# More seven-product pairs in the FFN down projections of a two-layer trunk, with weight parts and residual parked in DRAM

## The chip, the cores and the metric

The kernel runs on one core of one Trainium2 chip. The metric is device time in microseconds of one execution, the median of several runs; lower is better. Engines are named as in the profile: PE (TensorE, matrix products, with PEld its weight loads), DVE (VectorE), ACT (ScalarE), POOL (GpSimd) and SP (SyncE, which here only issues DMAs). Matrix products accumulate in PSUM, eight banks of 128 x 512 float32.

## The reference

Two layers over 256 positions of width 2048. Each layer is a token mixer (a gated MLP with spatial mixing in layer 0, latent attention in layer 1) and a gated FFN with a short causal convolution; each of the four sub-layers ends with a layer norm over the residual sum. What matters here:

```python
def layer_norm(x, g, b):
    mu = jnp.mean(x, axis=-1, keepdims=True)
    var = jnp.mean(jnp.square(x - mu), axis=-1, keepdims=True)
    return (x - mu) * lax.rsqrt(var + LN_EPS) * g + b

def conv_ffn(x, w_up, conv_w, conv_b, w_down):
    h = x @ w_up                                   # 2048 -> 2 * 5504
    h = causal_depthwise_conv(h, conv_w) + conv_b  # width 3
    a, g = jnp.split(h, 2, axis=-1)
    return (jax.nn.silu(g) * a) @ w_down           # 5504 -> 2048

for i in range(2):
    x = layer_norm(ALPHA * x + mixer_i(x), ln_mix_g[i], ln_mix_b[i])
    x = layer_norm(ALPHA * x + conv_ffn(x, ...), ln_ffn_g[i], ln_ffn_b[i])
```

All of it is in float32, and about 470 MB of weights are read once.

## The kernel before

*Products.* A float32 operand is split into a high part (a cast to fp32r, done by ACT) and a low part (operand minus high part, done by DVE). A product is three matmuls: high x high, low x high and high x low.

*Weights.* They come in the order of use as chunks of 1 MiB through SP's queue into a pool `big` of 22 slots of 1 MiB; the activations and the residual live in this pool too. `Feed` keeps the chunk list: `_load` (L76) issues the DMA into a tile `raw`, `_split` (L94) makes the parts `wh` and `wl` (L107, L108), `next` hands out the parts of the chunk now due and lets loads and splits run ahead of it.

*Up projection.* `ffn` runs 21 groups gi. A group takes four chunks (gi 21: two), each for four of the 16 k-tiles, into four banks; the convolution, the gate and the product `act` follow on ACT and DVE (L311, L313, L727 to L745).

*Down projection.* `down` takes its 43 k-tiles as 21 pairs and a single, in two halves of 1024 output columns (`halves`, in an order given by `BACK`). A pair is done for both 128-row blocks b and both 512-column pieces, in one of two ways. `eight` (a wide pair) takes the eight block products, 24 matmuls, into the four banks `DIRECT` = q3, p2, e, q4 (rows b=0 in the first two). `seven` uses the Strassen-Winograd scheme with seven block products, 21 matmuls; it needs sums of blocks of x (`Sums.make`, `combine`) and of the weights (`Feed._seven`: tile `ts`, and the parts wh, wl of 1536 columns and th, tl of 2048, L115 to L122), and four more banks `OWN`. When the last seven pair of a half is through, `rest` combines these banks and `fold` adds them into the residual. In the FFN, pairs 4, 10, 16, 22, 30 and 34 of each half are seven pairs. The last `SKEW` units of the second half are kept for `end(b, f)`, which runs them bank by bank.

*Residual and norm.* `Norm` holds the residual as two tiles of [128, 2048], one for each b, which stay in the pool through the up projection. `piece` adds a bank to the residual and takes its statistics; `start` makes mean and reciprocal deviation; `scale` normalises a piece (L574) and `put` transposes it (bank `lnt`, L587) and splits it into the next stage's operand `xhl` (L591, L594, L595). `boundary` writes out the order of these steps between a stage's end and the first group of the next (`upf` for an up projection, `mq` for the attention's first projection). Since `put` applies gain and bias only to the transposed copy, `restore` applies them to the residual later, in gi 3 to 10 or in the loop after mq, from tiles `lng` and `lnb` of 1 MiB each. In the last norm, `scale` applies gain and bias too (L576, L577) and stores to `out`.

*Order.* The code gives program order; a scheduler then orders the instructions of each engine and each DMA queue by its own estimates when the kernel is built, so the order on an engine can differ from that of the source. Slots of a pool are handed over by waits that it inserts.

Of the kernel before, what the change touches and what calls it, by code (L numbers as in the profile page):

```python
# [15 lines left out]
P = 128  # L16
# [38 lines left out]

BACK = {NF_GM: ((4, 10, 16, 22, 28, 34, 40), (11, 1, 2, 0, 4, 5, 7, 8, 10, 3, 6, 9), (5, 8)),
        NF_FF: ((4, 10, 16, 22, 30, 34), (10, 1, 2, 0, 4, 5, 7, 8, 3, 6, 9), ())}

# [10 lines left out]
class Feed:  # L69

    def __init__(self, nc, pool, chunks):
        self.nc, self.pool, self.chunks = nc, pool, chunks
        self.raw, self.parts = {}, {}
        self.loaded = self.split = self.used = 0  # L76

    def _load(self):
        ap, cols = self.chunks[self.loaded][:2]
        t = self.pool.tile([P, 2048], F32, tag="big", name=f"raw{self.loaded}")  # L80
        step = 512 if self.loaded == 0 else cols
        if len(ap.shape) == 3:
            self.nc.sync.dma_start(t.rearrange("p (k c) -> p k c", k=ap.shape[1]), ap)
        else:
            if self.loaded in (1, 2):
                step = 1024
            for o in range(0, cols, step):
                self.nc.sync.dma_start(t[:, o : o + step], ap[:, o : o + step])
                if self.loaded == 0 and o == step:
                    self.between[0]()  # L90
        self.raw[self.loaded] = t
        self.loaded += 1

    def _split(self):  # L94
        i = self.split
        cols, kind = self.chunks[i][1:]
        raw = self.raw.pop(i)
        if kind == "seven":
            self.parts[i] = self._seven(i, raw)
            self.split += 1  # L100
            return
        hi = self.pool.tile([P, 2048], F32R, tag="big", name=f"wh{i}")
        lo = self.pool.tile([P, 2048], F32R, tag="big", name=f"wl{i}")
        step = 512 if i == 0 else cols if kind == "wide" and i > 2 else 1024 if cols == 2048 else cols // 2
        for o in range(0, cols, step):
            c = slice(o, o + step)
            self.nc.scalar.copy(hi[:, c], raw[:, c])  # L107
            self.nc.vector.tensor_tensor(lo[:, c], raw[:, c], hi[:, c].bitcast(F32), ALU.subtract)  # L108
# [9 lines left out]
    def _seven(self, i, raw):  # L118
# [31 lines left out]
def trunk(ctx: ExitStack, tc: tile.TileContext, x, xT, gm_in, gm_wout, ffn_up, ffn_dn,  # L150
# [6 lines left out]
    st = ctx.enter_context(tc.tile_pool(name="st", bufs=4))  # L157
    ps = ctx.enter_context(tc.tile_pool(name="ps", bufs=8, space=bass.MemoryType.PSUM))

    def slot(shape, name, dt=F32):  # L160
# [8 lines left out]

    chunks = []  # L170
    n_up = ffn_up.shape[1]
# [5 lines left out]
    def back(w, n_k):  # L177

        for hf, units in enumerate(halves(n_k)):
            c = slice(hf * 1024, (hf + 1) * 1024)  # L180
            for u in units:
                if len(u) == 1:
                    chunks.append((w[u[0], :, c], 1024, "wide"))
                else:
                    chunks.append((w[u[0] : u[0] + 2, :, c].rearrange("k p c -> p k c"), 2048,
                                   "seven" if u[0] in BACK[n_k][0] else "wide"))

# [10 lines left out]

    feed = Feed(nc, big, chunks)

# [208 lines left out]
    def down(n_k, src, tag, ln, sums, skew=SKEW):  # L409


        ln.begin()
        quads, sevens = sums.quads, BACK[n_k][0]
        late = []
        for hf, units in enumerate(halves(n_k)):
# [5 lines left out]
            for i, u in enumerate(units):  # L421
# [94 lines left out]
    class Norm:  # L516


        def __init__(self, idx, res, last=False):
            self.idx, self.res, self.last, self.new = idx, res, last, None  # L520
            self.folded = set()

        def begin(self):
            if self.res is None:
                self.res = []
                for b in range(2):
                    t = slot([P, D], f"res{b}")
                    nc.sync.dma_start(t, x[b * P : (b + 1) * P, :])
                    self.res.append(t)
# [12 lines left out]

        def restore(self, b, f):

            c = slice(f * 512, (f + 1) * 512)
            r = self.res[b][:, c]
            nc.vector.tensor_tensor(r, r, self.g[:, c], ALU.mult)
            nc.vector.tensor_tensor(r, r, self.b[:, c], ALU.add)

        def fold(self, b, f, part):  # L550

            r = self.res[b][:, f * 512 : (f + 1) * 512]
            nc.vector.scalar_tensor_tensor(r, r, ALPHA, part, ALU.mult, ALU.add)
            self.folded.add((b, f))

        def piece(self, b, f, acc):
            r = self.res[b][:, f * 512 : (f + 1) * 512]
            if (b, f) in self.folded:
# [11 lines left out]
        def scale(self, b, f):  # L570
            c = slice(f * 512, (f + 1) * 512)
            r = self.res[b][:, c]
            if not self.last:
# [6 lines left out]
        def put(self, b, f):  # L580
# [4 lines left out]
            for j in range(4):  # L585
                o = f * 512 + j * P
                nc.tensor.transpose(t[:, j * P : (j + 1) * P], self.res[b][:, o : o + P], ident)  # L587
            y = tp.tile([P, 4, P], F32, tag="t2", name=f"lny{i}_{b}_{f}", bufs=6)
# [128 lines left out]

    ln = Norm(0, None)
    acc, end = down(NF_GM, pT, "wo", ln, sums)


# [12 lines left out]
    def ffn(layer, ln, acc, end, last):  # L734
# [25 lines left out]
        boundary(ln, acc, end, f"upf{layer}_", after)  # L760
        xhl, res = ln.new, ln.res
# [21 lines left out]
        ln = Norm(2 * layer + 1, res, last)  # L783
        return (ln, *down(NF_FF, act, f"dn{layer}", ln, sums, 4 if last else SKEW))
# [61 lines left out]
    xhl, res = ln.new, ln.res  # L846
    ln.rows()
    kvp = [(0, KVR // 2), (KVR // 2, KVR // 2)]
    acc = [[bank(f"mkv{b}_{f}") for f in range(2)] for b in range(2)]
    for c in range(6):  # L850
# [8 lines left out]
        if 1 <= c < 5:  # L859
            for f in range(2 * ((c - 1) % 2), 2 * ((c - 1) % 2) + 2):  # L860
                ln.restore((c - 1) // 2, f)
    kr2 = []
# [297 lines left out]
```

## Time and profile before

| what | value |
|---|---|
| runs | median 2494.65 us (2493.96 to 2495.05, three runs) |
| profiled execution | span 2492.6 us |
| PE, DVE, ACT, POOL busy | 2478.0, 1886.7, 1381.9, 2.9 us |
| DMA | 480.27 MB, mean 193 GB/s, 54.3% of 16 engines' span in the one queue of loads |
| granted PE clock | full in all 40 slices |
| layer 0's FFN | up projection to 1286.4 us, down projection 1286.4 to 1512.7 us |
| layer 1's FFN | down projection 2256.4 to 2482.2 us, then the last norm and the stores |

The span is the time from the first to the last instruction of the profiled execution; the runs are timed apart from it. An operand written `wl<-raw,wh 128x1024` means that the tile wl is written from raw and wh, in 128 partitions of 1024 elements. In the chain of waits each row is a stretch of the work that ended last, with start and length. In a view of windows each engine has its busy time in the stretch and its instruction count.

### The profile page before, as it was taken

To read this page: it belongs to the slowest core of one execution; us is meant where nothing else is said; L and a number is where in the kernel's file an instruction comes from. 1 tells how busy PE (TensorE), PEld (TensorE's weight loads), DVE (VectorE), ACT (ScalarE), POOL (GpSimd) and SP (SyncE) were. 2 spreads that over 40 slices of the span, in tenths; PEclk is the share of its full clock that TensorE was granted. 3 is DMA by queue.
4 is the path that set the end of the run, shared out by engine and by line. 5 is a ranking of instruction groups with operands and counts; after the bars stand their busy time and mean duration, and the time that the engine had idled before them with its cause. 6 is when DMAs were issued, how large, how long until landed. Compare 5 with 4: busy or idle time off the path is not lost.

```text
span 2492.6 us, 32653 instructions
## 1 busy us (share of the span) xinstructions
PE 2478.0 (99%) x13043; PEld 2131.8 (86%) x13043; DVE 1886.7 (76%) x2523; ACT 1381.9 (55%) x1880; POOL 2.9 (0%) x17
## 2 busy tenths in 40 slices
PE   9999999999999999999999999999999999999998
PEld 7888888888888888888888888988888888888886
DVE  7887866678888777666778997866497676669897
ACT  6565644445565755554655566565565555446553
POOL 0000000000000000000000000000000000000000
PEclk9999999999999999999999999999999999999999
DMA  7555554555566655555546674444465455555554
GB/s 281 217 188 204 200 182 158 184 191 198 186 212 227 219 187 203 186 186 180 192 154 201 219 245 171 168 153 166 157 230 193 167 203 180 181 180 178 209 192 181
DMA packets 86456, 480.27 MB, mean 193 GB/s; under 512 B 7712, under 2 KB 8480, under 8 KB 46752
## 3 DMA queue, kind: packets, MB, share of 16 engines
q1 hardware_dynamic: 86304, 478.19, 54.3%
q8 instruction: 102, 1.67, 0.3%
q14 instruction: 50, 0.41, 0.0%
HBM read 476.07 MB, written 2.10 MB: 192 GB/s over the span
## 4 chain that ended last, share of the span: by engine, by line
PE 98%; DVE 1%; DMA 0%; ACT 0%; issue 0%; SPq 0%; DVEq 0%; ACTq 0%
PE up L167 37%; PE u L167 11%; PE dn_q L167 9%; PE dn_p L167 6%; PE v_q L167 5%; PE wo_q L167 4%; PE mo L167 4%; PE v_p L167 3%; PE dn_e L167 3%; PE wo_p L167 3%; PE upf L167 2%; PE v_e L167 2%; PE wo_e L167 2%; PE mkv L167 1%; PE kn L167 1%; PE mq L167 1%
## 5 line engine op out<-in xcount | busy, mean ns | idle before, releaser
L108 DVE TENSOR_TENSOR wl<-raw,wh 128x1024 fp32r<-128x1024 f32 (+3 forms) x656 | 911.1, 1414 | 177.4 <-ACT wh L107 138.9
L107 ACT CAST wh<-raw 128x1024 fp32r<-128x1024 f32 (+3 forms) x656 | 771.2, 1207 | 299.7 <-DVE wl L108 119.8
L167 PE MATMUL up<-xhl,wh 128*128 128x512 f32 x2624 | 611.0, 390 | 0.0
L167 PEld LDWEIGHTS up<-xhl,wh 128*128 128x128 f32 x2624 | 487.4, 188 | 97.7
L167 PEld LDWEIGHTS up<-xhl,wl 128*128 128x128 f32 x2624 | 325.8, 192 | 6.4
L167 PE MATMUL up<-xhl,wl 128*128 128x256 f32 x2624 | 328.1, 283 | 0.0
L167 PE MATMUL u<-xhl,wh 128*128 128x512 f32 x768 | 183.8, 393 | 0.3 <-DVE h_u L313 0.2
L115 ACT CAST th<-ts 128x1536 fp32r<-128x1536 f32 x106 | 110.7, 1052 | 130.7 <-DVE ts L122 108.8
L167 PEld LDWEIGHTS u<-xhl,wh 128*128 128x128 f32 x768 | 141.3, 188 | 30.7 <-PE s L167 2.1
L116 DVE TENSOR_TENSOR tl<-ts,th 128x1536 fp32r<-128x1536 f32 x106 | 126.0, 1219 | 8.5 <-ACT th L115 7.6
L115 ACT CAST wh<-raw 128x1536 fp32r<-128x1536 f32 x53 | 78.5, 1482 | 53.5 <-DMA raw<-in_ffn_dn_dram 17.4
L167 PEld LDWEIGHTS u<-xhl,wl 128*128 128x128 f32 x768 | 95.6, 192 | 2.0
L167 PE MATMUL u<-xhl,wl 128*128 128x256 f32 x768 | 96.6, 283 | 0.0
L116 DVE TENSOR_TENSOR wl<-raw,wh 128x1536 fp32r<-128x1536 f32 x53 | 92.8, 1752 | 4.7 <-PE v_q L167 2.6
L167 PE MATMUL mo<-wh,oT 128*128 128x512 f32 x256 | 82.8, 404 | 0.0
L167 PE MATMUL v_q<-wh,xhl 128*128 128x512 f32 x264 | 82.2, 393 | 0.1
L167 PE MATMUL wo_q<-wh,woa 128*128 128x512 f32 x256 | 78.9, 389 | 0.0
L122 DVE TENSOR_TENSOR ts<-ts,raw 128x512 f32<-128x512 f32 x106 | 72.9, 688 | 1.6
L313 DVE TENSOR_TENSOR h_1a<-up,lo_1a 128x256 f32<-128x256 f32 x41 | 17.3, 421 | 73.6 <-ACT lo_1a L311 73.6
L313 DVE TENSOR_TENSOR h_0a<-up,lo_0a 128x256 f32<-128x256 f32 x41 | 17.3, 421 | 72.8 <-ACT lo_0a L311 72.8
L167 PE MATMUL dn_q<-wh,dn0a 128*128 128x512 f32 x232 | 71.7, 390 | 0.0
L167 PE MATMUL dn_q<-wh,dn1a 128*128 128x512 f32 x232 | 71.6, 389 | 0.0
(497 smaller groups left out, 3912.6 us busy)
## 6 DMA issues: line engine op xcount, KB each, us to landing
raw<-in_ffn_up_dram SPq DMA_DIRECT2D x172, 1024.0 KB, 4.7
raw<-in_gm_in_dram SPq DMA_DIRECT2D x93, 1024.0 KB, 4.8
raw<-in_ffn_dn_dram SPq DMA_DIRECT2D x84, 1024.0 KB, 5.1
raw<-in_gm_wout_dram SPq DMA_DIRECT2D x48, 1024.0 KB, 5.2
raw<-in_ml_out_dram SPq DMA_DIRECT2D x16, 1024.0 KB, 4.7
raw<-in_ml_b_dram SPq DMA_DIRECT2D x14, 1024.0 KB, 4.8
raw<-in_ml_kv_dram SPq DMA_DIRECT2D x5, 864.0 KB, 4.4
lng<-in_ln_rows_dram SPq DMA_DIRECT2D x4, 1024.0 KB, 5.0
```

Source lines behind the costliest of these rows:

```text
L107: self.nc.scalar.copy(hi[:, c], raw[:, c])
L108: self.nc.vector.tensor_tensor(lo[:, c], raw[:, c], hi[:, c].bitcast(F32), ALU.subtract)
L115: self.nc.scalar.copy(hi, raw)
L116: self.nc.vector.tensor_tensor(lo, raw, hi.bitcast(F32), ALU.subtract)
L122: add = lambda o, a, b: self.nc.vector.tensor_tensor(o, a, b, ALU.add)
L167: nc.tensor.matmul(o, l, r, start=start, stop=stop, skip_group_check=True)
L313: nc.vector.tensor_tensor(h, acc[:, 0:S], lo, ALU.add)
```

## The change

In `BACK` each kind of down projection gets a fourth entry, the pairs whose seven products use parked parts: 18, 28 and 32 for the FFN, in each half and each layer, none for the mixer's. So 12 wide pairs become seven pairs.

Their raw chunks are loaded and split in the up projection: `Feed.park` is a generator with four steps per chunk, of which one runs per up chunk from gi 2 on, so one parked chunk per gi in gi 2 to 7. It makes the sums and the parts as `_seven` does (in the pool), and stores wh, wl (0.75 MiB each), th and tl (1 MiB each) to DRAM tiles through POOL's queue. In the down projection `_fetch` takes the place of load and split for such a chunk and brings the four parts back through POOL's queue, from float32 in DRAM into fp32r tiles.

The residual is now two tiles of [128, 2, 1024], one for each half of the columns. In the up projection each is stored to DRAM through POOL's queue after gi 5 and gi 9 (`Norm.park`) and loaded through SP's queue eight units before the end of its half (`Norm.fetch`; for the first norm x is loaded in the same way). `restore` takes gain and bias by 512 columns into small tiles, at gi 2, 4, 6 and 8 or in the loop after mq, and serves both b; the slots of lng and lnb fall away except in the last norm.

```diff
-        NF_FF: ((4, 10, 16, 22, 30, 34), (10, 1, 2, 0, 4, 5, 7, 8, 3, 6, 9), ())}
+        NF_FF: ((4, 10, 16, 22, 30, 34), (10, 1, 2, 0, 4, 5, 7, 8, 3, 6, 9), (), (18, 28, 32))}
...
     def _load(self):
-        ap, cols = self.chunks[self.loaded][:2]
+        ap, cols, kind = self.chunks[self.loaded][:3]
+        if kind == "parked":
+            self.parts[self.loaded] = self._fetch(self.loaded)
+            self.loaded += 1
+            return
...
     def _split(self):
         i = self.split
-        cols, kind = self.chunks[i][1:]
+        cols, kind = self.chunks[i][1:3]
+        if kind == "parked":
+            self.split += 1
+            return
...
+    def park(self, i):
+
+        name = f"{i}"
+        tile = lambda n, dt: self.pool.tile([P, 2048], dt, tag="big", name=f"{n}{i}")
+        add = lambda o, a, b: self.nc.vector.tensor_tensor(o, a, b, ALU.add)
+        two = lambda a, o: a[:, o : o + 1024].rearrange("p (n c) -> p n c", n=2)
+        self.kept[i] = kept = {}
+
+        def store(n, t, cols):
+            d = self.dram.tile([P, cols], F32, tag=f"kept{n}{i}", name=f"kept{n}{i}", bufs=1)
+            self.nc.gpsimd.dma_start(d, t[:, 0:cols].bitcast(F32))
+            kept[n] = d
+
+        ap = self.chunks[i][0]
+        raw = tile("praw", F32)
+        self.nc.sync.dma_start(raw.rearrange("p (k c) -> p k c", k=ap.shape[1]), ap)
+        yield
+        t = tile("pts", F32)
+        add(two(t, 0), two(raw, 512), raw[:, None, 0:512].to_broadcast([P, 2, 512]))
+        add(t[:, 1024:1536], t[:, 0:512], raw[:, 1024:1536])
+        add(t[:, 1536:2048], t[:, 1024:1536], raw[:, 1536:2048])
+        yield
+        for n, src, o, cols in (("w", raw, 512, 1536), ("t", t, 0, 2048)):
+            hi, lo = tile(f"p{n}h", F32R), tile(f"p{n}l", F32R)
+            self._cast(hi[:, 0:cols], lo[:, 0:cols], src[:, o : o + cols])
+            store(f"{n}h", hi, cols)
+            store(f"{n}l", lo, cols)
+            if n == "w":
+                del raw, src, hi, lo
+                yield
+
+    def _fetch(self, i):
+
+        got = []
+        for n in ("wh", "wl", "th", "tl"):
+            d = self.kept[i].pop(n)
+            t = self.pool.tile([P, 2048], F32R, tag="big", name=f"f{n}{i}")
+            self.nc.gpsimd.dma_start(t[:, 0 : d.shape[1]], d)
+            got.append(t)
+        return got
...
-        quads, sevens = sums.quads, BACK[n_k][0]
+        quads, sevens = sums.quads, BACK[n_k][0] + BACK[n_k][3]
...
+                if i == n - 8:
+                    ln.fetch(hf)
...
+        def fetch(self, h):
+
+            if h in self.res:
+                return
+            t = slot([P, 2, 1024], f"res{self.idx}_{h}")
+            for b in range(2):
+                src = x[b * P : (b + 1) * P, h * 1024 : (h + 1) * 1024] if self.away is None else self.away[h][:, b, :]
+                nc.sync.dma_start(t[:, b, :], src)
+            self.res[h] = t
...
+        def park(self, h):
+
+            d = dram.tile([P, 2, 1024], F32, tag=f"res{self.idx}_{h}", name=f"resd{self.idx}_{h}", bufs=1)
+            nc.gpsimd.dma_start(d, self.res.pop(h))
+            self.put_away[h] = d
...
-        def restore(self, b, f):
-
-            c = slice(f * 512, (f + 1) * 512)
-            r = self.res[b][:, c]
-            nc.vector.tensor_tensor(r, r, self.g[:, c], ALU.mult)
-            nc.vector.tensor_tensor(r, r, self.b[:, c], ALU.add)
+        def restore(self, f):
+
+            row = []
+            for j in range(2):
+                t = tp.tile([P, 512], F32, tag="t2", name=f"lnp{self.idx}_{f}{j}", bufs=6)
+                src = ln_rows[2 * self.idx + j : 2 * self.idx + j + 1, f * 512 : (f + 1) * 512]
+                nc.sync.dma_start(t, src.to_broadcast([P, 512]))
+                row.append(t)
+            for b in range(2):
+                nc.vector.tensor_tensor(self.r(b, f), self.r(b, f), row[0], ALU.mult)
+                nc.vector.tensor_tensor(self.r(b, f), self.r(b, f), row[1], ALU.add)
...
+        units = [i for i in parked if feed.used < i < feed.used + 2 * n_up]
+
+        def park_all():
+
+            for i in units:
+                yield from feed.park(i)
+                yield
+
+        jobs = park_all()
         for gi in range(1, 22):
...
                 prod_a(acc, xhl, range(nk * c, nk * c + nk), hi, lo)
+                if gi > 1:
+                    next(jobs, None)
...
-            if gi == 1:
-                ln.rows()
-            if 3 <= gi < 11:
-                ln.restore((gi - 3) // 4, (gi - 3) % 4)
+            if gi in (2, 4, 6, 8):
+                old.restore(gi // 2 - 1)
+            if gi in (5, 9):
+                old.park((gi - 5) // 4)
```

More of the change, by code (lines that the diff above doesn't have):

```diff
@@ L167, in mm @@
         nc.tensor.matmul(o, l, r, start=start, stop=stop, skip_group_check=True)
-    chunks = []
+    chunks, parked = [], []
     n_up = ffn_up.shape[1]
@@ L184, in back @@
                 else:
-                    chunks.append((w[u[0] : u[0] + 2, :, c].rearrange("k p c -> p k c"), 2048,
-                                   "seven" if u[0] in BACK[n_k][0] else "wide"))
+                    kind = "seven" if u[0] in BACK[n_k][0] else "parked" if u[0] in BACK[n_k][3] else "wide"
+                    if kind == "parked":
+                        parked.append(len(chunks))
+                    chunks.append((w[u[0] : u[0] + 2, :, c].rearrange("k p c -> p k c"), 2048, kind))
     back(gm_wout, NF_GM)
@@ L196, in trunk @@
     back(ffn_dn[1], NF_FF)
-    feed = Feed(nc, big, chunks)
+    feed = Feed(nc, big, dram, chunks)
     idle = cpool.tile([P, 512], BF16, name="idle")
@@ L556, in piece @@
         def piece(self, b, f, acc):
-            r = self.res[b][:, f * 512 : (f + 1) * 512]
+            r = self.r(b, f)
             if (b, f) in self.folded:
@@ L571, in scale @@
             c = slice(f * 512, (f + 1) * 512)
-            r = self.res[b][:, c]
+            r = self.r(b, f)
             if not self.last:
@@ L585, in put @@
             for j in range(4):
-                o = f * 512 + j * P
-                nc.tensor.transpose(t[:, j * P : (j + 1) * P], self.res[b][:, o : o + P], ident)
+                c = slice(j * P, (j + 1) * P)
+                nc.tensor.transpose(t[:, c], self.r(b, f)[:, c], ident)
             y = tp.tile([P, 4, P], F32, tag="t2", name=f"lny{i}_{b}_{f}", bufs=6)
@@ L760, in ffn @@
         boundary(ln, acc, end, f"upf{layer}_", after)
-        xhl, res = ln.new, ln.res
+        xhl, old = ln.new, ln
+        jobs = iter([])
+        units = [i for i in parked if feed.used < i < feed.used + 2 * n_up]
[4 more added lines that the diff above has]
+        jobs = park_all()
         for gi in range(1, 22):
@@ L782, in ffn @@
                     sums.make(k)
-        ln = Norm(2 * layer + 1, res, last)
+        ln = Norm(2 * layer + 1, {}, old.put_away, last)
         return (ln, *down(NF_FF, act, f"dn{layer}", ln, sums, 4 if last else SKEW))
@@ L859, in trunk @@
         if 1 <= c < 5:
-            for f in range(2 * ((c - 1) % 2), 2 * ((c - 1) % 2) + 2):
-                ln.restore((c - 1) // 2, f)
+            ln.restore(c - 1)
     kr2 = []
```

26 lines of the change are left out of this document (12 added, 14 removed).

## The prediction

> **What bounds the kernel now.** I read the page first, its engine totals and its chain that ended last.
>
> ```profile
> span 2492.6 us, 32653 instructions
> PE 2478.0 (99%) x13043; PEld 2131.8 (86%) x13043; DVE 1886.7 (76%) x2523; ACT 1381.9 (55%) x1880; POOL 2.9 (0%) x17
> PE 98%; DVE 1%; DMA 0%; ACT 0%; issue 0%; SPq 0%; DVEq 0%; ACTq 0%
> ```
>
> TensorE (PE) is busy for 2478.0 of 2492.6 us and the chain is 98% PE. So a matmul taken away is worth its full issue time, and any new PE wait is paid in full. The sum is made against this execution; its span is 2.05 us under the median of 2494.65, so I add changes straight to the median.
>
> Next, the chain of waits in order of time, at the start of layer 0's down projection and at its end. Columns: start, length, what.
>
> ```profile
> 1286.44 1.36 PE dn_q L167 x6
> 1287.80 1.36 PE dn_p L167 x6
> ...
> 1504.08 4.08 PE dn_e L167 x18
> 1508.16 0.23 PE dn_q L167
> 1508.39 0.44 PE lnt L587 x4
> 1508.83 3.91 PE dn_q L167 x17
> 1512.74 0.44 PE lnt L587 x4
> 1513.17 2.75 PE mq L167 x12
> ```
>
> Six 512-column matmuls take 1.36 us, 0.2267 us each. At the stage's end the four transposes lnt slip in, and 17 matmuls of the last bank (3.91 us) cover the work that mq waits for: mq starts 0.43 us after the last of them, and that time is the second block of transposes. PE does not wait at this boundary.
>
> The windows show what is left of the other engines. Columns: stretch, PE, PEld, DVE, ACT, POOL, clock, DMA share, GB/s.
>
> ```profile
> 10.00:20.00 10.00, 10.00 (x46) 8.27 (x45) 7.67 (x15) 5.65 (x7) 0.00 (x0) 1.00 1.04 416
> 20.00:30.00 10.00, 10.00 (x46) 8.29 (x45) 7.42 (x9) 7.06 (x7) 0.00 (x0) 1.00 1.02 425
> 854.00:898.00 44.00, 44.00 (x256) 39.00 (x255) 43.68 (x64) 29.58 (x42) 0.00 (x0) 1.00 0.57 198
> 854.00:987.00 133.00, 133.00 (x768) 117.85 (x767) 107.83 (x167) 80.22 (x120) 0.00 (x0) 1.00 0.57 199
> 1300.00:1320.00 20.00, 20.00 (x90) 16.58 (x89) 20.00 (x24) 11.88 (x9) 0.00 (x0) 1.00 0.66 212
> 1300.00:1400.00 100.00, 100.00 (x443) 82.84 (x442) 87.28 (x83) 56.25 (x45) 0.00 (x0) 1.00 0.61 200
> ```
>
> The stretch 854 to 987 is gi 2 to 7 of layer 0's up projection (768 matmuls, six groups of 22.15 us), where the parked work goes. DVE is already 81% busy there. In the down projection (1300 to 1400) it is 87% busy, yet PE loses nothing.
>
> **The change, part by part.** *Matmuls.* A wide pair is 24 matmuls, a seven-product pair 21. Three pairs, two halves, two layers: 12 x 3 = 36 fewer, 36 x 0.2267 = 8.16 us. The order of the built programs agrees: the PE queue holds 8.1 us less work. This is the whole of the gain, since sums of x, casts and DVE work saved in the down stage hide under a PE that never waits.
>
> *The boundary from layer 0's down projection to mq.* The built order differs here. Before, rows b=0 close 18 + 17 matmuls ahead of rows b=1. After, the scheduler spreads the last units over the four banks; the first transpose stands behind the last dn matmul, and DVE holds the last piece of b=1, both its statistics and its aggregate ahead of the first scale of b=0. So the whole chain runs with PE idle. Its steps are in the timeline of before (DVE, then ACT):
>
> ```profile
> 1506.39 1.00 DVE L574 TENSOR_SCALAR res<-res,lnmv,lnrs 128x512 f32<-128x512 f32 x2
> ...
> 1512.77 0.69 DVE L559 TENSOR_TENSOR res<-res,dn_q 128x512 f32<-128x512 f32 x1 [1.02 <-PE dn_q L167]
> 1513.50 0.69 DVE L562 BATCH_NORM_STATS2 lnst<-res 128x6 f32<-128x512 f32 x1
> 1514.23 0.26 DVE L567 BATCH_NORM_AGGREGATE lnmv<-lnst 128x2 f32<-128x24 f32 x1
> 1514.94 0.16 DVE L276 RECIPROCAL lnrs<-lnrs_1q 128x1 f32<-128x1 f32 x1 [0.45 <-ACT lnrs_1q L274]
> 1515.14 0.55 DVE L574 TENSOR_SCALAR res<-res,lnmv,lnrs 128x512 f32<-128x512 f32 x1
> ```
>
> ```profile
> 1508.87 1.51 ACT L591 ACTIVATE lny<-lnt,lncol 128x128 f32<-128x128 f32 x4 [2.71 <-PE lnt L587]
> 1510.41 0.62 ACT L594 CAST xhl<-lny 128x512 fp32r<-128x512 f32 x1
> ```
>
> From the last dn matmul: piece and two statistics 0.7 + 0.6 + 0.7, reciprocal and aggregate 0.4, first scale 0.5, transposes to first ACT read 0.5 (1508.39 to 1508.87), ACT 1.54 + 0.62: mq's first matmul at about 5.6 us. Its second waits for the low part, which stands on DVE behind seven more scales (two in 1.0 us) and comes at about 7.1. Meanwhile PE does 15 transposes and one matmul, 1.9 us of work. Loss 7.1 - 1.9 = 5.2 us. Bounds: 3.5, the 3.9 us of matmuls that covered the last steps before, less 0.4 for transposes done meanwhile; 8, if each of six hand-overs waits as long as the reciprocal did (0.45). The two boundaries into the up projections hold their order, nothing there.
>
> *The tail.* The last normalisation has the same reordering, milder:
>
> ```profile
> 2471.33 0.69 DVE L559 TENSOR_TENSOR res<-res,dn_p 128x512 f32<-128x512 f32 x1 [0.40 <-PE dn_p L167]
> ...
> 2478.45 0.68 DVE L559 TENSOR_TENSOR res<-res,dn_e 128x512 f32<-128x512 f32 x1
> ...
> 2482.21 0.69 DVE L559 TENSOR_TENSOR res<-res,dn_q 128x512 f32<-128x512 f32 x1 [2.35 <-PE dn_q L167]
> ...
> 2483.66 0.26 DVE L567 BATCH_NORM_AGGREGATE lnmv<-lnst 128x2 f32<-128x24 f32 x1
> ```
>
> From 2471.33 the chain of b=0 takes DVE to 2478.45, 7.1 us, while PE has 48 matmuls left (10.9 us). In the new order 27 are left, 6.1 us, so DVE, not PE, is last. After 7.1 us come two pieces, then two statistics (0.6 + 0.7 + 0.6 + 0.7 = 2.6); the aggregate stands 9.7 - 6.1 = 3.6 us after PE's end instead of 2483.66 - 2482.19 = 1.5. Loss 2.1 us; no lower than 1.4, the piece and statistics that no longer run under PE.
>
> *Parking in the up projection.* Per unit DVE gets a 1024-wide sum, two of 512, and subtractions of 1536 and 2048. The down stage has all of these, in the groups by shape from 1310 to 1480; the last line is the 1024-wide cast of the up projection, grouped from 854 to 987:
>
> ```profile
> L108 DVE TENSOR_TENSOR wl<-raw,wh 128x2048 fp32r<-128x2048 f32 x23 | 52.5, 2289 | 7.1 <-ACT wh L107 6.3 <-PE dn_q L167 0.6
> L116 DVE TENSOR_TENSOR wl<-raw,wh 128x1536 fp32r<-128x1536 f32 x10 | 17.5, 1752 | 0.6 <-ACT wh L115 0.6
> L122 DVE TENSOR_TENSOR ts<-ts,raw 128x512 f32<-128x512 f32 x20 | 13.8, 688 | 0.3
> L122 DVE TENSOR_TENSOR ts<-raw 128x1024 f32<-128x1024 f32 x10 | 12.2, 1221 | 1.8 <-DMA raw<-in_ffn_dn_dram 0.9 <-PE dn_q L167 0.8
> ```
>
> ```profile
> L108 DVE TENSOR_TENSOR wl<-raw,wh 128x1024 fp32r<-128x1024 f32 x55 | 66.0, 1220 | 6.0 <-ACT wh L107 4.3 <-ACT s L744 0.8 <-issue 0.8
> ```
>
> 1.22 + 2 x 0.69 + 1.75 + 2.29 = 6.6 us; starts of instructions back to back lie 0.08 us closer, so 6.2. Six units: 37 us in 133. DVE had 107.83, of which 7 casts (8 us) only build up a lead: PE needs 48 there and 55 were made. 107.8 - 8 + 37 = 137 of 133: DVE is full and lives from its lead. It has one: from 854 to 898 it is 99% busy and gains. Price: nothing, if the lead that now grows to many chunks is merely eaten; 4 us a layer if it is short by the whole excess, 8 more if the waits for ACT stay (6.0 idle in the row above). I take 0, as the excess is under one chunk of 5.5 us, and keep +24 for both layers. DMA: a unit adds a 1.05 MB load and 3.67 MB of stores per 22.15 us, 213 GB/s on top of 199, 412 in all against 416 and 425 shown at the start. PE order leaves 26 to 40 us between a load's issue and its use, so I take 0.
>
> The residual's two stores, four loads and the eight row loads in place of lng and lnb move as many bytes, and DVE's restores are the same 16; the loads stand on SP ahead of weight loads that have the lead just named. Cost 0.
>
> *Fetching.* In the down stage POOL's queue brings 3.67 MB per unit. The trace of before has neither such a queue nor a transfer that changes type. Nearest rows: the 1 MiB weight load, alone and in the full first 60 us:
>
> ```profile
> raw<-in_ffn_dn_dram SPq DMA_DIRECT2D x84, 1024.0 KB, 5.1
> ```
>
> ```profile
> raw<-in_gm_in_dram SPq DMA_DIRECT2D x11, 1024.0 KB, 9.1
> ```
>
> By counting matmuls between what frees a slot and what reads it, the fetches have 10 to 21 us. The tightest place is the first half of each stage, where pairs 28, 30, 32, 34 follow each other: 2.62 MB must arrive up to pair 28's part th in 8.9 us, 295 GB/s. At 416 it has some 2.6 us in hand; at half of it, 208, it is 3.7 late, and the four units together (some 10 MB in 27 us) about 20 us late per layer. Weight loads behind the fetches keep 9.5 to 10.8 us where they had 13 or more, against 9.1 landing time in a full queue. Bounds: 0 and 40 for both layers; I take 2.5, a slip of about 0.6 at each of four half stages, nearer to the unhurried 5.1 us row.
>
> *Sum:* -8.2 + 5.2 + 2.1 + 0 + 2.5 = +1.6 us; 2494.65 + 1.6 = 2496.3, say 2496.5.
>
> **The rivals.** (a) *The gain stays.* Boundary and tail cost their lower ends, fetches nothing: -8.2 + 3.5 + 1.4 = -3.3, 2491.4; should the boundary's chain be hidden after all, -6.8, 2488. For it: PE never waits in the old down stage. Against it: the built order leaves no matmul to cover the chain, so the second needs an error in my reading of which instruction holds which.
>
> (b) *Slower, because parking saturates DVE*, in gi 2 to 7 of both layers. It decides once DVE's lead at gi 2 is under the excess. 4 to 12 us a layer: 2496.5 + 8 to 24, middle 2512. For it: 137 of 133. Against it: waits vanish when an engine falls behind.
>
> (c) *Slower, because fetches come late*, at pair 32 of each half. It decides below some 295 GB/s; at half rate 2496.5 + 40 - 2.5 = 2534. For it: the type change and the queue are new. Against it: the total is only 200 GB/s plus the fetches.
> Beside (c) stands a rule of the Trainium skill, "SBUF — State Buffer", the box on DVE blocking DMA: descriptors of a transfer issued on the POOL queue wait while DVE runs a two-port mode, as copies and tensor-with-scalar forms do. By that rule a DVE that is full (20.00 of 20.00 at 1300) would hold the fetches if those were its forms, with the price of (c); its work there is tensor-with-tensor, so by the rule's own list it would not. No run here shows it yet.
>
> That the change does less than it says is ruled out by the 36 matmuls counted.
>
> **How the numbers follow.** Forecast 0.50, its own range 2492 to 2503; (a) 0.13, (b) 0.22, (c) 0.15. A measurement here can tell about 0.2%, 5 us, from no change: 2489.7 to 2499.6. Faster: 0.10 of (a). Same: 0.40 of the forecast's 0.50 and 0.03 of (a). Slower: 0.10 + 0.22 + 0.15 = 0.47. The range 2489 to 2524 leaves out the lower part of (a) and most of (c), under 2 in 10.
>
> **What would show it.** PE matmul time down by 8 us. At the first boundary a gap of PE of about 5 us, ended by ACT and DVE, with the first mq after all dn matmuls. A last aggregate 3.6 us behind PE's last matmul. In gi 2 to 7 DVE near 100% and PE whole; PE gaps there ended by DVE speak for (b). PE gaps in the down stage ended by DMA of the parked parts speak for (c); landing times of 1 MiB parts well above 9 us would say so. The forecast is wrong if PE runs through the boundary or the sum of its gaps in the two stages passes some 8 us.

## The result, and the profile after

The changed kernel takes 2506.47 us (median of 4 runs, 2505.70 to 2507.53) beside 2494.85 us of the kernel before: ratio 1.0047, 95% interval 1.0035 to 1.0060. It is slower by 0.47%, 11.6 us. The profiled execution of after is the longest of its four (2507.53 us), so the stage times below add up to more than the difference of the medians. From its page: engine totals, the new queue, the parking's DMAs (columns of the last two: count, size, median us from issue to landing).

```profile
span 2505.8 us, 33085 instructions
PE 2478.4 (99%) x13007; PEld 2125.1 (85%) x13007; DVE 1934.7 (77%) x2601; ACT 1400.3 (56%) x1898; POOL 56.2 (2%) x117
...
q0 software_dynamic: 14400, 92.28, 9.3%
...
praw<-in_ffn_dn_dram SPq DMA_DIRECT2D x12, 1024.0 KB, 13.0
keptth<-pth POOLq DMA_DIRECT2D x12, 1024.0 KB, 10.8
```

PE has the 36 matmuls fewer (13043 to 13007), yet its busy time is the same. The ends of matmuls are modelled, so a short wait between two of them can count as busy time, and some matmuls ran at half clock (below). So the busy time does not tell; what tells is when the stages begin. From the first and last matmul of each stage in the two timelines:

| stretch | before, us | after, us | difference |
|---|---|---|---|
| start to the first upf matmul (gMLP mixer) | 804.4 | 803.0 | -1.4 |
| up projection, layer 0 | 481.8 | 481.8 | 0.0 |
| down projection, layer 0 | 226.5 | 228.5 | +2.0 |
| its last matmul to the first of mq | 0.2 | 5.8 | +5.6 |
| mq to the third projection (qr) | 51.8 | 54.3 | +2.5 |
| qr to the upf of layer 1 | 209.8 | 209.5 | -0.3 |
| up projection, layer 1 | 481.6 | 483.0 | +1.4 |
| down projection, layer 1 | 226.0 | 227.3 | +1.3 |
| tail | 10.5 | 12.5 | +2.0 |
| span | 2492.6 | 2505.8 | +13.1 |

The two down projections should each be 18 x 0.2267 = 4.1 us shorter; they are longer, so they have lost 6.1 and 5.4 us. The second loss is the boundary to mq with what follows, 8.1 us; the third the tail.

The boundary, from the DVE timeline of after (start, length, what):

```profile
1513.08 0.26 DVE L642 BATCH_NORM_AGGREGATE lnmv<-lnst 128x2 f32<-128x24 f32 x1
1513.40 0.69 DVE L634 TENSOR_TENSOR res<-res,dn_q 128x512 f32<-128x512 f32 x1
1514.01 1.28 DVE L637 BATCH_NORM_STATS2 lnst<-res 128x6 f32<-128x512 f32 x2
...
1515.50 1.85 DVE L649 TENSOR_SCALAR res<-res,lnmv,lnrs 128x512 f32<-128x512 f32 x4
1517.26 0.16 DVE L328 RECIPROCAL lnrs<-lnrs_1q 128x1 f32<-128x1 f32 x1
1517.45 1.92 DVE L649 TENSOR_SCALAR res<-res,lnmv,lnrs 128x512 f32<-128x512 f32 x4
1519.28 0.69 DVE L670 TENSOR_TENSOR xhl<-lny,xhl 128x512 fp32r<-128x512 f32 x1
```

The aggregate of rows b=0, which the first scale needs, is through at 1513.3; the scale (1515.50) stands behind the last piece and both statistics of rows b=1. (Ahead of b=0's own statistics DVE also does two splits of weights, 2.35 us.) The low part of the first xhl (1519.28) stands behind all eight scales. PE's waits from 1505 to 1530, by who ended them, name DVE and ACT (columns: us in total, times, longest):

```profile
PE lnt L662 <- DVE res L649: 2.7, 1, 2.7
PE mq L217 <- ACT xhl L669: 2.0, 1, 2.0
```

These waits bring a second loss with them. From 1518.4 to 1525.2 us the granted clock of PE is 0.50 (columns: stretch, PE, PEld, DVE, ACT, POOL, clock, DMA share, GB/s):

```profile
1519.00:1525.00 6.00, 5.86 (x17) 4.89 (x18) 3.89 (x5) 5.06 (x11) 0.00 (x0) 0.50 0.00 0
```

From 1521.08 to 1525.38 ten matmuls start, 0.43 us apart, where at 0.2267 they take 2.3 us: 2.0 of the 2.5 us in the row mq to qr. In before the clock is full there.

The loss in layer 0's down projection sits in two places. Counted from the starts of PE's matmuls, as what they lie further apart than 0.2267 us, PE loses 3.5 us at 60 to 100 us into the stage and 2.9 at 180 to 200, where the pairs 28 to 34 of the first and of the second half are done. (That is 0.4 more than the table has, whose stretch of before holds four transposes.) In layer 1 it is 3.4 and 2.0 us. The first place, from the windows of after (same columns):

```profile
1332.00:1345.00 13.00, 13.00 (x59) 10.76 (x58) 12.97 (x12) 7.29 (x7) 1.60 (x3) 1.00 0.60 196
1345.00:1350.00 5.00, 5.00 (x24) 4.14 (x23) 1.85 (x2) 2.86 (x2) 1.07 (x2) 1.00 1.07 414
1350.00:1355.00 5.00, 5.00 (x24) 4.14 (x23) 1.87 (x2) 0.00 (x0) 1.59 (x3) 1.00 1.04 396
1355.00:1360.00 5.00, 5.00 (x24) 4.14 (x23) 0.55 (x1) 0.57 (x1) 0.00 (x0) 1.00 1.05 381
1360.00:1365.00 5.00, 4.74 (x21) 3.49 (x20) 4.96 (x5) 4.23 (x5) 0.00 (x0) 1.00 1.07 425
1370.00:1380.00 10.00, 8.87 (x36) 6.16 (x35) 9.46 (x10) 7.14 (x8) 0.00 (x0) 1.00 0.89 299
```

Up to 1345 the DMA is 60% busy; then it is full for 20 us, and DVE, which was full, and ACT have little to do: they wait for weights. When these land DVE is full again, and PE, which has used up their lead, makes 36 matmuls in 10 us where 44 fit. The fetches stood on POOL's queue until PE gave slots free (timeline of POOL; in brackets the idle time and who ended it), and the weight load that the chain goes through took 12.39 us to land:

```profile
1342.22 0.54 POOL L179 DMA_DIRECT2D fwh<-keptwh  x1 [25.98 <-PE dn_q L217]
...
1352.42 0.54 POOL L179 DMA_DIRECT2D fwl<-keptwl  x1 [5.93 <-PE dn_q L217]
```

```profile
1346.94 12.39 DMA raw<-in_ffn_dn_dram
```

From 1342 to 1354 eight parts (two units, 7 MiB) and the weight loads ask for the DMA at once. In the second place the longest wait of PE in the stage is for a fetched part itself; it is the only one of the stage that a fetch ends:

```profile
1470.19 0.50 PE L217 MATMUL dn_q<-ftl,dn0xc 128*128 128x512 f32 x1 [1.20 <-DMA ftl<-kepttl]
```

The tail, from the DVE timeline of after:

```profile
2487.16 0.69 DVE L634 TENSOR_TENSOR res<-res,dn_p 128x512 f32<-128x512 f32 x1 [0.40 <-PE dn_p L217]
...
2494.28 0.68 DVE L634 TENSOR_TENSOR res<-res,dn_e 128x512 f32<-128x512 f32 x1
2494.87 0.68 DVE L634 TENSOR_TENSOR res<-res,dn_q 128x512 f32<-128x512 f32 x1
...
2496.79 0.26 DVE L642 BATCH_NORM_AGGREGATE lnmv<-lnst 128x2 f32<-128x24 f32 x1
```

PE ends at 2493.2 while DVE is still in the chain of b=0; the last aggregate stands 3.6 us behind PE's end.

And the parking itself, the same window as before (there 107.83 of DVE, 199 GB/s):

```profile
854.00:987.00 133.00, 133.00 (x768) 117.82 (x767) 121.55 (x169) 86.14 (x119) 11.69 (x22) 1.00 0.95 372
```

DVE goes to 91%, the DMA to 95%, and PE makes its 768 matmuls as before. The groups of this window show why DVE is not full (count, busy us, mean ns, idle before):

```profile
L116 DVE TENSOR_TENSOR wl<-raw,wh 128x1024 fp32r<-128x1024 f32 x44 | 52.9, 1218 | 0.4 <-ACT wh L115 0.4
...
L623 DVE TENSOR_TENSOR res<-res,lnp 128x512 f32<-128x512 f32 x4 | 2.7, 686 | 0.0
L622 DVE TENSOR_TENSOR res<-res,lnp 128x512 f32<-128x512 f32 x4 | 2.7, 688 | 0.0
```

It makes 44 of the casts, where before made 55, and 8 operations of the restores, where before had 16; the other eight stand ahead of the window.

### The profile page after: what moved, and what is told of

Same layout as the page of the kernel before. It is cut to its first block, busy times and chain, and to the rows that moved or that the text cites. A ratio compares the mean times of both kernels' runs of the same rounds, so it can differ in the third digit from the quotient of the medians.

```text
span 2505.8 us, 33085 instructions
## 1 busy us (share of the span) xinstructions
PE 2478.4 (99%) x13007; PEld 2125.1 (85%) x13007; DVE 1934.7 (77%) x2601; ACT 1400.3 (56%) x1898; POOL 56.2 (2%) x117
## 4 chain that ended last, share of the span: by engine, by line
PE 75%; issue 20%; DMA 2%; DVE 1%; POOL 0%; ACT 0%; SPq 0%; DVEq 0%; POOLq 0%; ACTq 0%
PE up L217 29%; PE u L217 11%; PE dn_q L217 6%; PE dn_p L217 5%; PE wo_q L217 5%; PE v_q L217 5%; PE v_p L217 3%; PE wo_p L217 3%; PE dn_e L217 2%; PE wo_e L217 2%; PE v_e L217 2%; PE upf L217 1%; PE s L217 1%; DMA raw<-in_ffn_dn_dram 1%; DMA keptwl<-pwl 0%
## 5 line engine op out<-in xcount | busy, mean ns | idle before, releaser
L116 DVE TENSOR_TENSOR wl<-raw,wh 128x1024 fp32r<-128x1024 f32 (+4 forms) x644 | 884.0, 1397 | 170.4 <-ACT wh L115 126.8
L115 ACT CAST wh<-raw 128x1024 fp32r<-128x1024 f32 (+4 forms) x644 | 747.4, 1193 | 272.4 <-DVE wl L116 81.2
L124 DVE TENSOR_TENSOR tl<-ts,th 128x1536 fp32r<-128x1536 f32 x106 | 126.2, 1219 | 18.8 <-ACT th L123 12.5
L130 DVE TENSOR_TENSOR ts<-raw 128x1024 f32<-128x1024 f32 x53 | 64.7, 1220 | 33.4 <-DMA raw<-in_ffn_dn_dram 28.0
L365 DVE TENSOR_TENSOR h_u<-u,lo_u 128x256 f32<-128x256 f32 x48 | 20.2, 421 | 52.2 <-ACT lo_u L363 52.2
L217 PEld LDWEIGHTS v_q<-wh,xhl 128*128 128x128 f32 x264 | 49.6, 189 | 12.3 <-ACT wh L115 2.1
L217 PE MATMUL v_p<-wh,xhl 128*128 128x512 f32 x192 | 59.6, 390 | 0.1
## 6 DMA issues: line engine op xcount, KB each, us to landing
keptth<-pth POOLq DMA_DIRECT2D x12, 1024.0 KB, 10.8
```

What stands on the lines that cost most here:

```text
L124: self.nc.vector.tensor_tensor(lo, raw, hi.bitcast(F32), ALU.subtract)
L130: add = lambda o, a, b: self.nc.vector.tensor_tensor(o, a, b, ALU.add)
L217: nc.tensor.matmul(o, l, r, start=start, stop=stop, skip_group_check=True)
L365: nc.vector.tensor_tensor(h, acc[:, 0:S], lo, ALU.add)
```

## The experiments

Each time stands beside runs of the kernel before on the same chip (2494.3 to 2494.4 us). "Edges" are ordering edges for the scheduler, without a wait. Stage times are of one profiled execution each.

**order.** In boundary (for mq) and in the last norm; `at[0]` is PE's last matmul or transpose so far, `s` and `p` the last instruction of `scale` and `put` (the lines that note these are left out):

```diff
+        hold = tc.issue_after if tag == "mq" else lambda i: nullcontext()
         for f in fs:
-            end(0, f)
+            with hold(at[0]):
+                end(0, f)
             ln.piece(0, f, acc[0][f])
         ln.start(0)
         ln.scale(0, 0)
-        ln.scale(0, 1)
-        end(1, fs[0])
-        ln.put(0, 0)
-        ln.piece(1, fs[0], acc[1][fs[0]])
-        end(1, fs[1])
+        s = ln.scale(0, 1)
+        with hold(at[0]):
+            end(1, fs[0])
+        with hold(at[0]):
+            p = ln.put(0, 0)
+        with hold(s):
+            ln.piece(1, fs[0], acc[1][fs[0]])
+        with hold(p):
+            end(1, fs[1])
...
-            end(b, f)
+            with tc.issue_after(at[0]):
+                end(b, f)
```

> The changed kernel with one thing more: ordering edges (no waits) that keep, at the boundary to mq and at the end, the late matmuls bank by bank (q3, p2, e, q4), the first transposes ahead of the last bank, and DVE's pieces of rows b=1 behind the first two scales of b=0. Nothing is computed differently. By the traces the boundary and the first projections behind it take 7.9 us more than before and the tail 2.2. If the order is the cause, about 9 of these 10 come back: 2497.5 us (2496 to 2500), mq starts 0.5 us after the last dn matmul and the last aggregate stands 1.5 us behind PE's end. Rival: the order only mirrors weights that land late; then PE waits inside the last units instead and the time stays at 2504 or more.

Measured: 2500.97 us (ratio 1.0029, 1.0019 to 1.0039), span 2498.5. The last dn matmul to mq: 0.2 us; mq to qr: 51.9; tail 10.5. The boundary's 8.1 us and the tail's 2.0 are back, and so is the full clock, so the order is their cause. But layer 1's down projection grew from 227.3 to 232.0 us: there the rival holds, and the time lies between the two forecasts. In the chain of this run, near that stage's end, PE stands behind a weight load that took 12.60 us:

```profile
2449.24 12.60 DMA raw<-in_ffn_dn_dram
...
2461.94 1.93 ACT wh L115
```

Behind these waits the clock is at half again, from 2467.3 to 2470.7: eight matmuls take 3.5 us where 1.8 would do, 1.7 of the 4.7. That in the scheduler's own order PE had other banks to go on with while those weights came is a reading of the two orders; no run took it apart.

**spread.** `(), (18, 28, 32))` becomes `(), (6, 18, 28))`.

> The changed kernel with the parked pairs 6, 18, 28 in place of 18, 28, 32: as many matmuls, fetches and bytes, but no row of four seven-product pairs 28, 30, 32, 34. Theory: the 11.6 us that the two down projections lose come from a burst, in which eight fetches and the weight loads between them share the DMA rate (about 420 GB/s at 1342 to 1366 us) so that weight loads take 12.4 us to land. Then most of the 11.6 goes: 2498 to 2501. Rival: a fetch costs its stall wherever it stands (the queue, the change of type, or its four slots): 2505 to 2508.

Measured: 2506.93 us (1.0050, 1.0035 to 1.0065). The theory of the neighbours 28 to 34 does not hold: the down projections take 229.5 and 227.7 us, no less than with 18, 28, 32. The loss moved in part. At 60 to 100 us into the stage it fell from 3.5 to 2.3 us in layer 0 and from 3.4 to 1.0 in layer 1, though a weight load (from 1347.26) still lands only after 11.47 us. In its place each layer loses 0.7 us in the first 40 us and 1.2 to 1.6 at 120 to 160, near the parked pair 6 of each half, and some 3.0 us at 160 to 180, up to the second half's pair 28 (one wait there, of 1.2 and 2.0 us, is for its part tl).

**fetch_sp.**

```diff
-            self.nc.gpsimd.dma_start(t[:, 0 : d.shape[1]], d)
+            self.nc.sync.dma_start(t[:, 0 : d.shape[1]].bitcast(F32), d)
```

> The changed kernel with the parts fetched through SP's queue as plain float32 bytes, not through POOL's queue with a change of type. If POOL's queue or the change of type makes the fetches late, the down projections' stalls go and the time falls to 2495 to 2500. If the DMA rate shared in the burst is the cause, the same bytes come at the same time: 2505 to 2510, perhaps worse, as weight loads now stand behind fetches in one queue.

Measured: 2505.62 us (1.0046, 1.0029 to 1.0063), down projections 227.7 and 227.2 us. The boundary loses its time here too (5.5 us to mq). Neither POOL's queue nor the change of type makes the fetches late.

**unused.** Parked, but not used in the down projection:

```diff
-                    kind = "seven" if u[0] in BACK[n_k][0] else "parked" if u[0] in BACK[n_k][3] else "wide"
-                    if kind == "parked":
+                    kind = "seven" if u[0] in BACK[n_k][0] else "wide"
+                    if u[0] in BACK[n_k][3]:
                         parked.append(len(chunks))
...
-        quads, sevens = sums.quads, BACK[n_k][0] + BACK[n_k][3]
+        quads, sevens = sums.quads, BACK[n_k][0]
```

> The changed kernel with all of its parking (sums, casts, stores, residual), but the down projections take pairs 18, 28 and 32 as wide pairs from their raw weights as before, so nothing parked is fetched back but the residual. Theory: parking in the up projection costs little (1.4 us over both layers by the traces) and the order at the boundary is nearly that of before: 2495 to 2498. Rival: full DVE and DMA in the up projections cost much and show only at the next boundary: 2500 or more.

Measured: 2494.27 us (0.9999, 0.9990 to 1.0008). The up projections take 481.8 and 482.2 us, the down projections 226.5 and 225.9, the step to mq 0.2, the tail 11.0. All sums, casts, stores and the residual's way through DRAM together cost less than a measurement can tell; 2.0 us gained in the first mixer (see the next section) stand against 1.4 lost in the second up projection, the tail and behind mq. With the same parking load the boundary to mq keeps its time and the tail nearly so. So it is not the parking that made the scheduler change the order, but what this run leaves out, the fetches or the twelve further seven-product pairs; no run parts these two.

**order_mq.** The edges at the boundary alone.

> The changed kernel with the ordering edges at the boundary to mq alone, not at the end. With edges at both places the boundary gave back all of its 8.1 us, but layer 1's down projection grew by 4.7 us while the tail gave back 2.2. If the two places do not touch each other: 2506.5 - 8.1 = 2498.4 us (2497.5 to 2499.5), layer 1's down projection 227 us and the tail 12.6 us as in the changed kernel. Rival: layer 1 grew for another reason than the edges at the end; then 2500 or more.

Measured: 2500.27 us (1.0024, 1.0015 to 1.0033). By stages the expectation holds: the boundary at 0.2 us, layer 1's down projection 227.4, the tail 12.5, span 2497.4, which is 8.4 under that of after. The median is 1.9 us over the number expected, just inside the rival's 2500 or more, and 6.2 under after's. Runs of this kernel scatter from 2499.0 to 2502.4, more than those of before (2493.9 to 2494.8), and the profiled execution (2499.2) is one of the shorter ones, that of after the longest of its four; what the longer runs lose, and where, is not on record.

**sums_order.** As the last; only the sums are parked, and raw and sums loaded:

```diff
-        for n, src, o, cols in (("w", raw, 512, 1536), ("t", t, 0, 2048)):
...
+        store("ts", t, 2048)
...
+        t = self.pool.tile([P, 2048], F32, tag="big", name=f"fts{i}")
+        self.nc.gpsimd.dma_start(t, self.kept[i].pop("ts"))
+        return t
```

`_split` then treats the pair as a seven pair without the three sums.

> As the last, but only the sums of weight blocks (tile ts, 1 MiB) are made and parked in the up projection; in the down projection raw and ts are loaded and the four parts are made there as for the other seven-product pairs. A parked pair then loads 2.1 MB in place of 3.67 and takes six slots instead of four, and costs DVE and ACT there more. If bytes in a full DMA stretch cause the down projections' stalls (about 10 us over both), most of them go: 2490 to 2494 us. If slots of the pool cause them, or DVE: as the last or slower, 2498 and more.

Measured: 2494.96 us (1.0002, 0.9993 to 1.0012). Between the two: the down projections take 226.5 and 226.1 us where 222.4 and 221.9 are their matmuls. Beside order_mq the stall falls from 6.3 and 5.5 us to about 4 each, not away. Fewer bytes do this although DVE and ACT have more to do; but from its fetch to its split a pair now also holds two slots (raw and ts), not four, so the run does not part bytes from slots.

**one18_order.** `(), (18,))`, edges at the boundary.

> As order_mq, with pair 18 alone parked, one in place of three per half. Twelve matmuls fewer than before (2.7 us). If each fetched pair costs its own stall (about 10 us over 12 of them, 0.85 each): 4 x 0.85 = 3.4 us of stalls, and with 1.9 gained at the start and 2.2 lost in the tail about 2495.4 us. If only the cluster of 28 to 34 stalls, there are no stalls: 2492 us.

Measured: 2493.44 us (0.9996, 0.9987 to 1.0006). Both down projections are 1.4 us shorter than before, the six matmuls each: one parked pair per half is hidden whole. The number for no stalls, 2492, was missed for the tail, which is 14.1 us here, 3.6 over before.

**bufs21.** The pool `big` with 21 slots in place of 22.

> The changed kernel with a pool of 21 slots in place of 22. If the fetches come late because their slots come free late, one slot less makes each later by about one more chunk and the time grows by several us: 2509 or more. If the DMA rate alone sets the stalls: 2505 to 2508.

Measured: 2530.30 us (1.0142, 1.0126 to 1.0157), 24 us over after. Down projections 232.9 and 229.4 us, 4.4 and 2.1 more than with 22 slots; the up projections, in which the parking takes slots, 5.9 and 7.0 more. But the first mixer, in which no weight parts are parked or fetched, grows by 4.5 us too, and PE has three further stretches of 3.4 us at half clock. So a slot less costs in stages without fetches too, and the run does not show that the fetches' slots are what makes the stalls; the kernel before was not run with 21 slots.

**one18_full, two_full, one28_order.** Pair 18 with edges at both places; pairs 18 and 28 with edges at both; pair 28 with edges at the boundary.

> Pair 18 alone parked, with the ordering edges at the boundary to mq and at the end. With the boundary's edges alone each down projection was 1.4 us shorter than before, all that its six matmuls are worth, but the tail 3.7 us longer, since only 30, 22 and 11 matmuls were left behind the first three banks. If the weights of the last units land in time, as with one pair they may, the tail comes back: 2493.4 - 3.7 = 2489.7 us (2489 to 2491). Rival: the last units' weights are late as with three pairs and edges, and PE waits in the last units: 2492 to 2495.

Measured: 2492.31 us (0.9992, 0.9983 to 1.0001). This is the rival's range. Tail 10.9, but layer 1's down projection 226.9 where 224.6 are its matmuls: the edges at the end give 3.2 us back and cost 2.3.

> Pairs 18 and 28 parked, edges at both places. A further 2.7 us of matmuls less than the last. If pair 28 does not stall: 2487 to 2488. If its fetch, next to the weight loads of the seven-product pairs 30 and 34, stalls as the cluster with three pairs did (some 2.5 us per half stage): 2489 to 2496, no better than one pair.

Measured: 2494.17 us (1.0000, 0.9990 to 1.0009). Layer 0's down projection is 224.9 us, 1.5 shorter than before, where 2.7 are its matmuls; the second pair is worth under 0.2 us there, as PE loses 1.2 in the first half at 60 to 100 us. Layer 1's, which has the edges at the end, takes 228.8, 1.9 more than with one pair; a stretch of 3.4 us at half clock lies in it.

> Pair 28 alone parked, edges at the boundary to mq alone: the twin of the run with pair 18 alone, with the pair at another place. If what stalls is a fetch next to the seven-product pairs 30 and 34, whose six slots each and weight loads are wanted at the same time, the down projections stall here, 0 to 2.5 us longer than before each: 2495 to 2499. If a single fetch is hidden anywhere, each is 1.4 us shorter as with pair 18, and the time is 2493 to 2494.

Measured: 2492.76 us (0.9994, 0.9985 to 1.0003), both down projections 1.4 us shorter. At neither of the two places tried does a single pair stall. With two pairs the first half stalls, with three both halves do.

**one_late.** As one18_full, with `if left == 6: ln.prep()` changed to `left == 4`.

> Pair 18 alone parked, edges at both places, and the last norm's gain and bias (lng, lnb, 2 MiB) asked for two units later, so that they stand on SP's queue behind the last two weight loads and not ahead of them. With lng and lnb ahead, layer 1's down projection took 226.9 us where 224.6 are its matmuls, and PE waited in the last units. If the two loads made the last weights late, these 2.3 us come back: 2492.3 - 2.3 = 2490.0 us (2489 to 2491). Rival: the last weights wait for slots or for DVE, not for the two loads: 2492 or more; or lng is then late itself, and the tail grows.

Measured: 2492.21 us (0.9991, 0.9982 to 1.0000); layer 1's down projection 226.6 us. The rival holds: lng and lnb ahead in the queue were not the cause. The last weight loads go out when PE frees a slot (2440.25) and land by 2447.4; from there to PE's waits (1.1 and 0.3 us, both ended by DVE, at 2460 and 2462) the chain is DVE's work. Which of the two, slots or DVE, sets the loss is open. This and one18_full are the fastest kernels here, 2.0 to 2.2 us under before, at the edge of what the intervals tell from no change.

## Why the prediction came out as it did

The measured 2506.5 lies inside the whole range, on the side that was given the largest chance, but 10 us over the forecast and outside the forecast's own range (2492 to 2503). By the sign that the text set itself (gaps in the two stages above some 8 us) the forecast is wrong: the down projections alone lose 11.5. Of the 0.47 for slower, 0.22 belonged to (b), which the runs exclude, and 0.15 to (c), whose mechanism they do not bear out. So that the side was met is in part luck; the fetching was taken 9 us too small, and the boundary 3. By steps:

- *Matmuls, -8.2.* Right as a count (13043 to 13007), and one parked pair does bring its 1.4 us per stage (one18_order). Nothing of the 8.2 is left in after, as the fetches' stalls took it.
- *Boundary, +5.2.* The mechanism is shown: order takes it away whole. mq's first matmul was expected 5.6 us behind the last dn matmul; the stage table has 5.8. The size fell short, 8.1: mq to qr took another 2.5 us, of which 2.0 are matmuls at half clock (granted 0.50 for 6.8 us). The sum took every matmul behind the gap at its full rate; that a gap of PE can be followed by a slower clock stood in it nowhere.
- *Tail, +2.1.* Measured 2.0, the aggregate 3.6 us behind PE's end and 27 matmuls left behind the last bank of b=0, both as worked out; order restores it.
- *Parking, 0.* Right: unused. The excess of DVE, 137 of 133 us, did not come about. DVE was busy 121.55 us in that window. Most of the difference is 44 casts where the sum put 48 (4.9 us), eight restore operations that stand ahead of the window (5.5) and the last 2048-wide subtraction behind it (2.3). Rival (b) is excluded: PE made 768 matmuls in the window as before. Layer 1's up projection had +1.4 us in after, +0.6 in unused, up to +2.2 with 22 slots (spread) and 0 in seven of the other profiled runs: not settled, and small.
- *Fetching, +2.5.* This is the mis-sized term: 6.1 + 5.4 = 11.5 us (4.1 that should have been gained in each, plus +2.0 and +1.3). The text took a slip of 0.6 us for each half stage, near the row of the unhurried load of 5.1 us; the four half stages lost 2.0 to 3.5. It had looked at the weight loads behind the fetches and given them 9.5 to 10.8 us against 9.1 of landing; the one that the chain goes through took 12.39. And it left DVE and ACT out: mostly not the fetched parts end PE's waits (one of 1.2 us, for ftl) but ACT and DVE, whose weights came late and who, once full, could not make up the lost lead.
- *Rival (c)* had the stage right and the mechanism wrong. The fetches are not at half rate: the DMA moves 381 to 425 GB/s while they land, and through SP's queue it is the same. The same run answers the rule of the Trainium skill, "SBUF — State Buffer", the box on DVE blocking DMA: taken off POOL's queue, whose descriptors the rule is about, the fetches came no sooner, which agrees with the reading that tensor-with-tensor forms don't block. The sign of (c), landing times well above 9 us, came in part: 9.9 and 11.9 us for the 1 MiB parts.
- *Not in the sum:* the first mixer's stretch is 1.2 to 2.0 us shorter in every run with 22 slots, in unused too, all of it in its down projection wo (first wo matmul to first upf: 254.4 us before, 252.5 in after), where x is now loaded late and by halves. That this is the cause was only argued; no run took it apart.

What the runs show of the 11.5 us is where they are lost and that they need more than one parked pair in a half. How they divide between the slots that set when a fetch goes out, the DMA rate in the burst, and DVE's work for the further seven-product pairs stays open. One slot less costs 4.4 and 2.1 us in the down projections (bufs21), but also 4.5 us in the first mixer; 1.6 MB less per fetched pair gives 2.2 and 1.3 us back (sums_order beside order_mq), but changes the slots as well. A larger pool, and fetches asked for earlier, were not tried.

## What to carry to other kernels

Where DVE and ACT run just ahead of a full PE out of a fixed pool, price a transfer that replaces their work by the stretch in which it lands, and not by the mean bandwidth: the mean over layer 0's down projection was 277 GB/s, and the DMA was full for 20 us all the same. Here, in layer 0, one fetched pair in half a stage was hidden whole, a second was worth under 0.2 us, and a third cost more than it saved (228.3 us in order, 224.9 in two_full).

Look at the built order around every stage boundary after a change of a stage's inputs, even where the code there is unchanged: a changed order cost 8 us at a boundary that the diff hardly touches. And look at the granted clock behind each new gap of PE, as the gap may not be the whole price: 2.0 of these 8 us are matmuls at half clock.

An ordering edge repairs such a place only if the data really is there by then. Where it was not, the edges at the end turned an order loss into waits: 2.0 us back and 4.7 lost in order, 3.2 and 2.3 in one18_full.

## What the runs showed of the hardware

A fetch from DRAM into fp32r tiles on POOL's queue, the kind that changes type, ran at the full rate (DMA share 1.04 to 1.07 at 381 to 425 GB/s, mixed with SP's loads) and took no longer than the same bytes without a change of type on SP's queue: the median landing of the 1 MiB parts in layer 0's down projection was 9.9 and 11.9 us on POOL's queue, 9.9 and 11.8 us on SP's.

```profile
fth<-keptth POOLq DMA_DIRECT2D x6, 1024.0 KB, 9.9
ftl<-kepttl POOLq DMA_DIRECT2D x6, 1024.0 KB, 11.9
```

```profile
fth<-keptth SPq DMA_DIRECT2D x6, 1024.0 KB, 9.9
ftl<-kepttl SPq DMA_DIRECT2D x6, 1024.0 KB, 11.8
```

(The first two rows are from after, the other two from fetch_sp; columns are count, size and median us from issue to landing.) In the 133 us of layer 0's parking, stores to DRAM among the loads (372 GB/s in all, 199 before) did not slow PE, which made its 768 matmuls as before.

The granted clock fell to 0.50 behind some waits of PE and not behind others. In after it did so at 1518.4 us for 6.8 us, when PE had waited 2.7 us (to 1516.0) and was in the next wait, of 2.0; in order at 2467.3 for 3.4 us, behind waits of 0.5 and 1.9 us. A single wait of 1.2 us (after, at 1470) and one of 1.4 (one18_full, at 2460) were followed by none. At 0.50 a matmul of 512 columns started every 0.43 us, at the full clock every 0.2267.
